# Weight sums in DRAM, in other groups and tied to other instructions, in a two-layer trunk

## The chip, the cores and the metric

One core of a Trainium2 chip runs the whole kernel. The metric is the device time of one execution in microseconds (us); lower is better. The engines are named as in the profile: PE (matmuls), PEld (PE's weight loads), DVE (vector), ACT (activation), POOL (general vector work, and here the issuer of software DMAs), SP (issuer of the loads). Each engine works through its own instruction queue in order, and waits for others by semaphores.

## The reference

The model has one sequence of 512 rows with 1024 features, and two layers. Layer 0 mixes with gated linear attention (queries, keys, values, gates and a decay, in chunks), layer 1 with a three-branch sparse attention (compressed, selected and windowed keys). Both add an attention over a memory of 256 rows, project the result with `w_out`, and then run a feed-forward part with a short convolution:

```python
h = h + jnp.concatenate([main.astype(xn.dtype), mo.astype(xn.dtype)], axis=-1) @ w_out[i]
h = h + conv_ffn(rmsnorm(h, norm_ffn[i]), w_up[i], conv_w[i], conv_b[i], w_down[i])
```

All is float32. The feed-forward part is `(silu(a) * b) @ w_down` with `a, b` the halves of the convolved `x @ w_up`, 2816 wide each.

## The kernel before

**Matmuls in three.** Every float32 factor is split into a high and a low part (ACT makes the high one, DVE the rest), and a product is three matmuls: high by high, low by high, high by low. Weights come in blocks of 128 x 1024 floats (512 KB): SP loads one (`wraw`), ACT and DVE split it (`wh`, `wl`), PE uses it. PE is given its order by hand wherever the code ties each matmul to the one before.

**Products with seven in place of eight.** Much of the two feed-forward parts multiplies 2 x 2 blocks with seven products instead of eight. These need sums of the four quarters of a weight block. The sums don't depend on the data, so the kernel lets POOL form them in DRAM by DMA beside the other work, in the array `qsum`. There are 35 such blocks, and each takes five transfers, which the code calls stages and this text calls **sums** alike:

- stages 0 and 1: a plain copy of two quarters each (512 KB) from the input `in_qd` to `qsum`;
- stage 2: two quarters of the input added to the first two (512 KB, an accumulating DMA);
- stages 3 and 4: one quarter of `qsum` added to another (256 KB each). Stage 3 needs stages 1 and 2, stage 4 needs stage 3.

`self.jobs` lists all 175 in order, in groups of blocks: stage 0 of each block of a group, then stage 1 of each, and so on. `pace(ins, n)` (line 284) takes the next `n` from the list, issues them on POOL's queue, and ties each to the instruction `ins` of another engine, so that it can't go out before. A sum that needs another waits on POOL for its landing, and there are eight semaphores for these DMAs in turn, so each also waits for the one eight places before. POOL's own work stands in the same queue: what is behind a waiting sum waits too.

**The order of the work**, with the calls of `pace` that matter here:

- Layer 0: queries and keys in six projections (`queries_keys`, line 706; from the fourth on two sums each); the memory's keys and values (two sums after each of two projections); the memory's two query projections (two each); the **value projection** `glav` beside the attention over the memory (one sum every eight steps, eight in all). Beside it POOL casts four pieces of the decays (`las`, line 759) for a DVE subtraction (line 761), which stands in DVE's queue ahead of work of the attention over the memory (`mP`).
- The gated linear attention in eight pieces (three sums each). POOL makes there the factor `oss` of a norm (lines 906 and 907), which DVE needs at line 911; behind that stand the merges `C`, and behind those ACT's copies `v` (line 900) that free PE's bank `po`.
- `w_out` (line 1023, line 1032 its matmuls) for layer 0, blocks 3 to 7: two sums each, tied to `low_ins`, the DVE instruction that has split the block's weights.
- The feed-forward part of layer 0, with sums tied to ACT's convolutions. Its start, and that of layer 1's, needs `rc` (line 426): DVE makes a mean of squares from PE's column sums, POOL raises it to the power -1/2, and PE transposes it (line 432) between two runs of 12 matmuls of the second up-projection.
- Layer 1: keys with four sums, the values of the sparse branches (`values` in `others`, line 2116, seven sums), then six double steps of scores and values. POOL multiplies the softmax weights `P` there (line 2061), which PE then transposes (line 1996).
- `w_out` for layer 1: eight blocks, two sums each, tied as above. Then the second feed-forward part and the output.

## Time and profile before

| what | value |
|---|---|
| time, median of 3 runs | 1247.51 us (1245.46 to 1250.63) |
| the profiled execution's own time | 1246.41 us |
| its span, first to last instruction | 1244.6 us |
| PE busy | 1217.1 us (98%) |
| DVE, ACT, POOL busy | 950.5, 694.4, 255.5 us |
| mean granted PE clock | 0.989 |
| software DMAs (the sums and two more) | 25408 packets, 75.74 MB |
| loads by SP | 61068 packets, 155.90 MB |

Rows of a timeline read: start, length, engine, line, instruction, out<-in, how many; in brackets the engine's idle time before it and what ended that. Rows of waits read: who waited for whom, us in total, times, the longest. Issuing a DMA on POOL is shown with the time that POOL spends on it, not with the transfer's. Line numbers are those of the kernel before; in the changed one those behind the list are three or four higher.

### The profile page before, as it was taken

Reading aid. Unit: us, or ns where it says so; the run is one execution under the profiler, and the core shown is the slowest. Engines: PE = TensorE matmul, PEld = TensorE weight load, DVE = VectorE, ACT = ScalarE, POOL = GpSimd, SP = SyncE. Lnnn points to the kernel's source line nnn. Section 1 sums busy time; section 2 is a strip of 40 time slices with the busy share of each in tenths; the row PEclk is TensorE's granted clock in tenths of the full one; section 3 lists DMA queues with packets and bytes.
Section 4 is the critical chain, followed back from the end, with each engine's and each line's share of the span. In section 5 each row is a group of like instructions: output and inputs, shape, how many; then the busy total and the mean of one; then the engine's idle time right before and its main releaser. Section 6 shows DMA issues by size and latency. Waiting matters only on the chain.

```text
span 1244.6 us, 20732 instructions
## 1 busy us (share of the span) xinstructions
PE 1217.1 (98%) x7657; PEld 1056.2 (85%) x7657; DVE 950.5 (76%) x1723; ACT 694.4 (56%) x1321; POOL 255.5 (21%) x356
## 2 busy tenths in 40 slices
PE   9989999999999999999999999699999999999998
PEld 6878788888889999899888788688888888988886
DVE  7755777689868888778768577685599888888785
ACT  7646455456545555556625677574456555555554
POOL 1221344210111110110122355673111111100000
PEclk9989989999999999999999999899999999999999
DMA  8786769966877876987765733733977988975544
GB/s 289 217 204 164 127 169 171 230 195 209 185 186 222 216 189 201 272 196 228 219 195 188 162 94 98 170 96 109 225 186 180 267 230 213 229 211 168 179 128 152
DMA packets 88385, 235.47 MB, mean 189 GB/s; under 512 B 10111, under 2 KB 13984, under 8 KB 87772
## 3 DMA queue, kind: packets, MB, share of 16 engines
q1 hardware_dynamic: 61068, 155.90, 39.3%
q0 software_dynamic: 25408, 75.74, 30.9%
q10 hardware_dynamic: 1808, 2.51, 0.6%
q8 instruction: 60, 0.98, 0.3%
q14 instruction: 41, 0.34, 0.1%
HBM read 222.01 MB, written 79.74 MB: 242 GB/s over the span
## 4 chain that ended last, share of the span: by engine, by line
PE 88%; DMA 5%; DVE 2%; ACT 1%; POOL 1%; issue 1%; SPq 0%; POOLq 0%; ACTq 0%; DVEq 0%
PE acc L1256 15%; PE acc L1152 11%; PE acc L1158 10%; PE acc L1032 5%; PE acc L385 4%; PE po L1995 3%; DMA qsum<-qsum 3%; PE sc L1332 3%; PE acc L1332 2%; PE po L1332 2%; PE sc L1521 2%; PE po L1521 2%; PE acc L1995 2%; PE acc L782 2%; PE acc L1521 2%; PE po L403 2%
## 5 line engine op out<-in xcount | busy, mean ns | idle before, releaser
L201 DVE TENSOR_TENSOR wl<-wraw,wh 128x1024 fp32r<-128x1024 f32 (+2 forms) x128 | 147.4, 1162 | 21.4 <-ACT wh L201 20.0
L201 ACT ACTIVATE wh<-wraw 128x1024 fp32r<-128x1024 f32 (+2 forms) x128 | 128.1, 1007 | 49.8 <-issue 14.8
L201 DVE SCALAR_TENSOR_TENSOR hc<-acc,taps,hc 128x511 f32<-128x511 f32 (+1 forms) x144 | 107.7, 748 | 48.2 <-ACT hc L201 45.9
L349 ACT ACTIVATE wh<-wraw 128x1024 fp32r<-128x1024 f32 x80 | 84.5, 1057 | 91.7 <-PE acc L1032 33.3
L350 DVE TENSOR_TENSOR wl<-wraw,wh 128x1024 fp32r<-128x1024 f32 x80 | 102.7, 1284 | 19.6 <-ACT wh L349 19.0
L282 POOL DMA_DIRECT2D qsum<-qsum x70 | 60.0, 913 | 240.0 <-ACT hc L201 104.7
L201 ACT ACTIVATE hc<-acc,taps 128x512 f32<-128x512 f32 x72 | 55.9, 777 | 91.5 <-DVE acc L201 38.2
L1256 PE MATMUL acc<-xh,wh 128*128 128x512 f32 x272 | 105.9, 390 | 0.0
L1256 PE MATMUL acc<-xh,wl 128*128 128x512 f32 x272 | 105.9, 389 | 0.0
L1256 PE MATMUL acc<-xl,wh 128*128 128x512 f32 x272 | 105.8, 389 | 0.0
L280 POOL DMA_DIRECT2D qsum<-in_qd x70 | 39.3, 563 | 275.8 <-ACT hc L201 163.3
L1152 PE MATMUL acc<-xl,wh 128*128 128x512 f32 x208 | 81.0, 389 | 0.0
L1152 PE MATMUL acc<-xh,wl 128*128 128x512 f32 x208 | 81.0, 389 | 0.0
L1152 PE MATMUL acc<-xh,wh 128*128 128x512 f32 x208 | 80.9, 389 | 0.0
L2061 POOL TENSOR_TENSOR P<-P,ssm 128x256 f32<-128x256 f32 (+3 forms) x48 | 64.9, 1373 | 1.8
L1256 PEld LDWEIGHTS acc<-xh,wh 128*128 128x128 f32 x272 | 51.1, 188 | 10.7 <-issue 0.4
L1256 PEld LDWEIGHTS acc<-xl,wh 128*128 128x128 f32 x272 | 51.1, 188 | 10.6
L1256 PEld LDWEIGHTS acc<-xh,wl 128*128 128x128 f32 x272 | 51.1, 188 | 10.3
L2053 ACT ACTIVATE P<-P,smn 128x128 f32<-128x128 f32 (+3 forms) x96 | 53.3, 557 | 10.1 <-DVE smn L2051 9.0
L282 POOL DMA_DIRECT2D qsum<-in_qd x35 | 29.5, 913 | 126.2 <-ACT hc L201 96.4
L1152 PEld LDWEIGHTS acc<-xl,wh 128*128 128x128 f32 x208 | 39.0, 188 | 8.2
L1152 PEld LDWEIGHTS acc<-xh,wl 128*128 128x128 f32 x208 | 39.0, 188 | 7.8
(631 smaller groups left out, 3816.3 us busy)
## 6 DMA issues: line engine op xcount, KB each, us to landing
wraw<-in_wp SPq DMA_DIRECT2D x122, 512.0 KB, 4.7
qsum<-in_qd POOLq DMA_DIRECT2D x105, 512.0 KB, 6.9
qsum<-qsum POOLq DMA_DIRECT2D x70, 256.0 KB, 7.3
wraw<-qsum SPq DMA_DIRECT2D x30, 512.0 KB, 5.3
wraw<-in_qd SPq DMA_DIRECT2D x30, 512.0 KB, 5.1
wraw<-qsum SPq DMA_DIRECT2D x51, 256.0 KB, 5.5
wraw<-in_qd SPq DMA_DIRECT2D x26, 256.0 KB, 4.3
strip<-vecd SPq DMA_DIRECT2D x12, 448.0 KB, 4.1
```

Source lines behind the costliest of these rows:

```text
L201: ins = f(*a, **kw)
L282: return self.nc.gpsimd.dma_start(to, what, accum_op=ALU.add)
L349: self.split_ins = nc.scalar.activation(wh, raw, AF.Copy)
L350: self.low_ins = nc.vector.tensor_tensor(out=wl, in0=raw, in1=wh.bitcast(F32), op=ALU.subtract)
L1032: nc.tensor.matmul(banks[m], a[:, o], b, start=k == 6 and i == 0, stop=k == 5 and i == 2)
L1152: pe(nc.tensor.matmul(dst, w[a][:, o], self.x[k][b], start=k + n == 0, stop=k == KC - 1 and n == 2))
L1158: pe(nc.tensor.matmul(dst, w[a][:, o], (X if n < 4 else T)[n][k][x], start=first and k + i == 0, stop=k == 3 and i == 2, skip_group_check= ...
L1256: pe(nc.tensor.matmul(pu[half], a[:, o], self.x[k][b], start=k == 0 and n == 0, stop=k == KC - 1 and n == 2))
L1332: pe(nc.tensor.matmul(dst, a[:, o], b, start=first and n == 0 and i % 2 == 0, stop=stop and n == 2, skip_group_check=True))
L1521: pe(nc.tensor.matmul(bank[i][:, c], a[:, ts], b[:, c], start=first and n == 0, stop=stop and n == 2, skip_group_check=True))
L1995: mm = lambda *args, **kw: pe(nc.tensor.matmul(*args, **kw))
L2061: nc.gpsimd.tensor_tensor(out=P, in0=P, in1=f[:, i, :].unsqueeze(2).to_broadcast([128, 2, 128 * t + 128]), op=ALU.mult)
```

## The change

Three edits. The first two groups of the list hold six blocks each (60 sums), all later ones three as before. The fourth of the query and key projections issues no sums. `w_out` ties its sums to the last matmul of the same block instead of to the split of its weights, and issues two per block in layer 0 and three per block in layer 1; the values of the sparse branches issue none.

```diff
--- before.py
+++ after.py
@@ -234,7 +234,10 @@
             for i, j in enumerate(FAST[l]):
                 blocks += [self.upb(l, j), self.downb(l, n - 1 + i)]
             blocks += [self.downb(l, p) for p in range(n - 1 + len(FAST[l]), NJ // 2)]
-        self.jobs = [(b, n) for i in range(0, len(blocks), 3) for n in range(5) for b in blocks[i:i + 3]]
+        self.jobs = []
+        while blocks:
+            some, blocks = blocks[:6 if len(self.jobs) < 60 else 3], blocks[6 if len(self.jobs) < 60 else 3:]
+            self.jobs += [(b, n) for n in range(5) for b in some]
 
     def t(self, pool, shape, tag, dt=F32, bufs=None):
         self.n += 1
@@ -710,7 +713,8 @@
                     else:
                         qp = self.ps("sc" if i == 3 else "acc")
                         self.projA(qp, self.wget(self.W[("glak", "glaq")[r]][j]))
-                        self.pace(self.move, 2)
+                        if i > 3:
+                            self.pace(self.move, 2)
                     sc = DK ** -0.5 if r else 1.0
                     for lo, hi, dst in ((0, DK, qk[:, :, r, j, :]), (DK, 128, qk[32 * j:32 * j + 32, :, r, 3, :])):
                         nc.vector.scalar_tensor_tensor(out=dst, in0=qp[lo:hi].rearrange("p (c t) -> p c t", c=4), scalar=sc,
@@ -1029,7 +1033,7 @@
             for k in ks:
                 o = slice(128 * k, 128 * k + 128)
                 for i, (a, b) in enumerate(((wh, main[k][0]), (wl, main[k][0]), (wh, main[k][1]))):
-                    nc.tensor.matmul(banks[m], a[:, o], b, start=k == 6 and i == 0, stop=k == 5 and i == 2)
+                    self.move = nc.tensor.matmul(banks[m], a[:, o], b, start=k == 6 and i == 0, stop=k == 5 and i == 2)
 
         ws, banks = {}, {}
         for m in range(lead):
@@ -1042,7 +1046,7 @@
                 banks[m] = self.ps("acc")
                 part(m, (6, 7))
             part(m, range(6))
-            self.pace(self.low_ins, 2)
+            self.pace(self.move, 2 + l)
             self.residual(m, banks[m], 4 + l)
 
 
@@ -2123,8 +2127,6 @@
                     for i, _ in enumerate(values()):
                         if i == 16:
                             run(q, 3)
-                        if i % 5 == 0:
-                            self.pace(self.move)
                         yield
                     c0 = compressed(0)
                     ahead_c.append(c0)
```

The program's order of instructions moves on POOL alone (on DVE one subtraction `las` changes places with two neighbours).

POOL, from the first sums to the casts of `las` in layer 0, before:

```order
L280 DMA qsum_81<-in_qd 128x1024 x6
L426 TENSOR_TENSOR rcm_544<-rcm_544,mhalf_110 128x2
L282 DMA qsum_81<-in_qd 128x1024 x3
L282 DMA qsum_81<-qsum_81 128x512 x6
L759 CAST las_121<-las_121 64x384
L280 DMA qsum_81<-in_qd 128x1024
L759 CAST las_121<-las_121 64x384
```

The same place now:

```order
L283 DMA qsum_81<-in_qd 128x1024 x4
L429 TENSOR_TENSOR rcm_542<-rcm_542,mhalf_110 128x2
L283 DMA qsum_81<-in_qd 128x1024 x8
L285 DMA qsum_81<-in_qd 128x1024
L763 CAST las_121<-las_121 64x384
L285 DMA qsum_81<-in_qd 128x1024
L763 CAST las_121<-las_121 64x384
```

Ahead of the first cast stood six copies, three sums of stage 2 and six of stages 3 and 4; now twelve copies and one sum of stage 2 stand there.

POOL in the fourth double step of the sparse attention, before (`Pc` and `cf` belong to the compressed branch, `ssm` and `P` to the softmax weights):

```order
L2089 TENSOR_TENSOR cf_8612<-cf_8612,gates_6344 128x8
L2090 TENSOR_TENSOR Pc_8487<-Pc_8487,cf_8612 128x256
L282 DMA qsum_81<-qsum_81 128x512 x3
L280 DMA qsum_81<-in_qd 128x1024
L282 DMA qsum_81<-qsum_81 128x512
L2058 TENSOR_TENSOR ssm_8536<-ssm_8536,gates_6344 128x4
L280 DMA qsum_81<-in_qd 128x1024
L2061 TENSOR_TENSOR P_1463_8537<-P_1463_8537,ssm_8536 128x512
L2061 TENSOR_TENSOR P_1474_8618<-P_1474_8618,ssm_8536 128x768
```

and now:

```order
L2093 TENSOR_TENSOR cf_8603<-cf_8603,gates_6342 128x8
L2094 TENSOR_TENSOR Pc_8478<-Pc_8478,cf_8603 128x256
L2062 TENSOR_TENSOR ssm_8527<-ssm_8527,gates_6342 128x4
L2065 TENSOR_TENSOR P_1463_8528<-P_1463_8528,ssm_8527 128x512
L2065 TENSOR_TENSOR P_1474_8609<-P_1474_8609,ssm_8527 128x768
L2076 MEMSET Pc_8780 128x8
```

The six sums between these products are gone; all sums of this part stand behind the last product.

POOL from the last products `P` to `rc` of the second feed-forward part, before:

```order
L2061 TENSOR_TENSOR P_1620_9214<-P_1620_9214,ssm_9213 128x512
L2061 TENSOR_TENSOR P_1625_9228<-P_1625_9228,ssm_9213 128x768
L280 DMA qsum_81<-in_qd 128x1024 x2
L282 DMA qsum_81<-in_qd 128x1024 x3
L282 DMA qsum_81<-qsum_81 128x512 x3
L426 TENSOR_TENSOR rc_9752<-rc_9752,mhalf_110 128x4
L282 DMA qsum_81<-qsum_81 128x512 x3
```

and now:

```order
L2065 TENSOR_TENSOR P_1620_9205<-P_1620_9205,ssm_9204 128x512
L2065 TENSOR_TENSOR P_1625_9219<-P_1625_9219,ssm_9204 128x768
L283 DMA qsum_81<-in_qd 128x1024 x4
L285 DMA qsum_81<-in_qd 128x1024 x3
L285 DMA qsum_81<-qsum_81 128x512 x6
L283 DMA qsum_81<-in_qd 128x1024 x6
L285 DMA qsum_81<-in_qd 128x1024 x3
L285 DMA qsum_81<-qsum_81 128x512 x2
L429 TENSOR_TENSOR rc_9751<-rc_9751,mhalf_110 128x4
L285 DMA qsum_81<-qsum_81 128x512 x4
```

Eight sums stood between the last `P` and `rc`; now 24 do.

## The prediction

> **What bounds the kernel now.** I read the engines' busy time first, then TensorE's waits, then who held the engine that was waited for.

> ```profile
> PE 1217.1 (98%) x7657; PEld 1056.2 (85%) x7657; DVE 950.5 (76%) x1723; ACT 694.4 (56%) x1321; POOL 255.5 (21%) x356
> ```

> PE is busy for 98% of the span. A change that moves only DMAs on POOL's queue can therefore win only from PE's few waits, and lose only by making new ones. The view of PE's waits has three that matter:

> ```profile
> PE pt L1996 <- POOL P L2061: 9.6, 1, 9.6
> PE pt L585 <- DVE mP L576: 4.7, 1, 4.7
> PE po L782 <- ACT v L900: 3.4, 1, 3.4
> ```

> The view by stretches, one stretch for each wait, from the last matmul before it to the end of the reduced clock behind it, gives the whole price (columns: length, then busy time of PE, PEld, DVE, ACT, POOL, then the granted clock, DMA share and GB/s):

> ```profile
> 81.55:90.41 8.86, 4.17 (x13) 3.50 (x13) 7.09 (x14) 2.83 (x10) 1.05 (x3) 0.62 0.75 151
> 152.58:162.09 9.51, 6.11 (x19) 5.14 (x19) 6.69 (x27) 4.54 (x16) 3.87 (x8) 0.64 0.75 165
> 797.21:810.63 13.42, 3.78 (x13) 3.19 (x14) 3.95 (x12) 3.52 (x13) 6.41 (x9) 0.62 0.93 208
> ```

> Length less PE busy is the wait: 4.69, 3.40 and 9.64 us. PE's work after each wait runs at half clock (a granted 0.62 to 0.64 over a stretch is half for most of it), so half of the 4.17, 6.11 and 3.78 us is lost too: 2.1, 3.05 and 1.9. I call them A (6.8 us), B (6.45) and C (11.5); together **24.8 us**.

> All three lead to POOL. For A and B the waits of DVE name it:

> ```profile
> DVE las L761 <- POOL las L759: 6.9, 1, 6.9
> DVE v L911 <- POOL oss L907: 6.4, 2, 6.0
> ```

> POOL runs its queue in order, and a weight sum whose earlier stage has not landed holds whatever stands behind it. POOL's timeline at A, at B and at C:

> ```profile
> 51.69 1.79 POOL L282 DMA_DIRECT2D qsum<-in_qd  x2 [0.21 <-issue]
> ...
> 63.35 0.81 POOL L282 DMA_DIRECT2D qsum<-qsum  x1 [7.38 <-DMA qsum<-in_qd]
> 67.24 0.84 POOL L282 DMA_DIRECT2D qsum<-qsum  x1 [3.07 <-DMA qsum<-in_qd]
> 71.51 0.82 POOL L282 DMA_DIRECT2D qsum<-qsum  x1 [3.43 <-DMA qsum<-in_qd]
> 75.02 0.81 POOL L282 DMA_DIRECT2D qsum<-qsum  x1 [2.69 <-DMA qsum<-qsum]
> 77.47 0.81 POOL L282 DMA_DIRECT2D qsum<-qsum  x1 [1.64 <-DMA qsum<-qsum]
> 80.22 0.83 POOL L282 DMA_DIRECT2D qsum<-qsum  x1 [1.94 <-DMA qsum<-qsum]
> 81.10 0.50 POOL L759 CAST las<-las 64x384 fp32r<-64x384 f32 x1
> ...
> 147.81 0.81 POOL L282 DMA_DIRECT2D qsum<-qsum  x1 [2.02 <-DMA qsum<-qsum]
> 148.69 0.19 POOL L906 TENSOR_SCALAR oss<-oss 128x2 f32<-128x2 f32 x1
> ...
> 793.84 2.51 POOL L282 DMA_DIRECT2D qsum<-qsum  x3
> ...
> 803.41 0.81 POOL L282 DMA_DIRECT2D qsum<-qsum  x1 [6.51 <-DMA qsum<-qsum]
> ...
> 805.74 2.48 POOL L2061 TENSOR_TENSOR P<-P,ssm 128x512 f32<-128x512 f32 x2
> ```

> At A the cast that DVE needs stands behind nine sums in which each third waits for the one three places ahead. At B the factor `oss` stands behind the same kind of wait. At C one sum waits 6.51 us, and the product P that PE is to transpose stands behind it.

> **The change part by part.** *Groups of six* (the first 60 sums). A sum now needs a stage issued six or more places earlier. The cast of `las` stands behind 13 sums: eight plain copies of stages 0 and 1, which wait for nothing but their matmuls, four copies that wait for the copy eight places before, and one sum of stage 2, which waits for the fifth copy. That one goes out where POOL stands at 51.69 now, and has until 71 to land. None is a sum of the stages 3 and 4 that hold POOL from 63.35 to 80.22. POOL comes to the cast when the first matmuls of the value projection release the sum before it, right behind the second query projection, whose result DVE reads at 71.10:

> ```profile
> 71.10 0.69 DVE L497 SCALAR_TENSOR_TENSOR qf<-sc,rb 128x512 f32<-128x512 f32 x1 [0.35 <-PE sc L385]
> ```

> So the cast comes at some 72 to 73 instead of 81.10. DVE begins to wait for it at about 74.7 (its wait of 6.9 ends with the cast, at 81.6). So A goes: **-6.8**. At B the sums ahead of `oss` are of stages 3 and 4, but their sources were all issued in the value projection, two pieces of work earlier. POOL then makes `oss` as soon as ACT has its squares, and DVE's 6.0 us wait, longer than PE's 3.4, goes: **-6.45**. It isn't paid back by blocks that come too late: the first formed block is read at 257.7, and its last needed stage is then the 19th of 175 sums, issued in the value projection. At the end the last sum goes out at 1098.7 and the last formed block is read at 1140.1, 41 us later.

> ```profile
> L282 POOL DMA_DIRECT2D qsum<-qsum x70: 805/824/1477, 63.3 to 1098.7; - x70
> ...
> L291 SPq DMA_DIRECT2D wraw<-qsum x9: 319/327/327, 257.7 to 1140.1; - x9
> ```

> *No sums at the fourth projection, none beside the sparse values.* Two and seven sums fewer at those places. They cost PE nothing there, so I count 0. Every sum behind them is two places later in the first feed-forward part and one in the second, some 5 to 10 us of the 41 just named.

> *Second output projection*: 24 sums instead of 16, each three tied to the end of a block's own matmuls, not to the split of its weights, which had run ahead into the attention. So no sum stands between the products P: C goes, **-11.5**.

> But all 24 now stand between the last P and `rc` of the second feed-forward part. There POOL had 14.30 us to spare:

> ```profile
> 862.38 1.07 POOL L280 DMA_DIRECT2D qsum<-in_qd  x2 [11.50 <-DVE wl L350]
> 866.51 1.70 POOL L282 DMA_DIRECT2D qsum<-in_qd  x2 [3.07 <-DVE wl L350]
> 870.60 0.81 POOL L282 DMA_DIRECT2D qsum<-in_qd  x1 [2.40 <-DVE wl L350]
> 877.51 0.83 POOL L282 DMA_DIRECT2D qsum<-qsum  x1 [6.10 <-DMA qsum<-in_qd]
> ...
> 886.42 0.81 POOL L282 DMA_DIRECT2D qsum<-qsum  x1 [3.02 <-DMA qsum<-in_qd]
> 901.53 1.03 POOL L426 TENSOR_TENSOR rc<-rc,mhalf 128x4 f32<-128x4 f32 x1 [14.30 <-DVE rc L425]
> ```

> and PE needs `rc` soon after it can be made, since its transposes stand between two runs of 12 matmuls (the chain of waits: start, length, what):

> ```profile
> 856.49 7.25 PE acc L1032 x31
> ...
> 867.82 27.20 PE acc L1032 x120
> 895.02 5.44 PE acc L1256 x24
> 901.25 2.89 PE acc L385 x12
> 904.57 2.76 PE acc L385 x12
> ```

> The first block's 18 matmuls end at about 859.5 (half of the 36 that end at 863.6), the last block's at 895.0. How long do 24 sums take? They queue in the DMA engines one behind another, so I price each kind by the distance of two landings. Stage 2 (512 KB added): 67.24 to 63.35 and 71.51 to 67.24, 4.1 us; here, 877.51 to 886.42 for two, 4.45. Stages 3 and 4 (256 KB added): 75.02, 77.47, 80.22, so 2.6. Copies (512 KB), from three that went out 0.5 us apart at 931.8:

> ```profile
> DMA to landing us min/median/max: 5.6/6.7/8.3
> ```

> (8.3 - 5.6 + 1.0) / 2 = 1.85 us, with 3.7 us ahead of the first. The last sum before `rc` may go out when the sum three places ahead, the 21st, has landed. These 21 are 10 copies, 5 of stage 2 and 6 of stages 3 and 4: 18.5 + 20.5 + 15.6 = 54.6 us. With 3.7 from 859.5 that is 917.8; the issue (0.82) and `rc` (1.03) end at 919.7. PE is free at 904.1 (901.25 + 2.89), so it waits **15.6 us**, and loses about 2.3 behind it at half clock (mean of 2.1, 3.05 and 1.9): **+17.9**. Nothing fills this hole: every matmul left needs `rc`'s row or stands behind it.

> Bounds: all software transfers of the POOL queue together (packets, MB, share of the span) show

> ```profile
> q0 software_dynamic: 25408, 75.74, 30.9%
> ```

> which is 384.6 us for 177 transfers, 2.17 us each, against 2.6 for my mix of 15 sums (38.9 / 15). At that rate 54.6 becomes 45.6 and the wait 6.6. With 4.45 for stage 2 and 10% more for the rest it is 59.8, and the wait 20.8. I take the middle because the rows at 63 to 80 and at 866 to 886 have the same mix of sums and weight loads. [...]

> The sum against the profiled execution's own 1246.41: 1246.4 - 6.8 - 6.45 - 11.5 + 17.9 = **1239.6 us**. That execution is 1.1 us under the median of 1247.51, of which the forecast is 0.6% less.

> **The rivals.** *The sums drain in time.* If the 21 need under 38.3 us (901.5 - 859.5 - 3.7), `rc` isn't late: 1246.4 - 24.8 = 1221.6. For it: the loads of the next weights stop once PE stands, which frees the engines. Against: it needs 30% less than the rows. [...]

> *Groups of six don't free the cast and `oss`.* If POOL is as late as now at A and B, only C is won: 1246.4 - 11.5 + 17.9 = 1252.8. For it: twelve copies now stand close together at 43 to 71, beside the weight loads. Against: none of the sums ahead of the cast needs a source younger than 8 places.

> *Slower: the DMA engines are overbooked.* At the second feed-forward part's start, just behind 895.0, SyncE stores h, when copies and stage-2 sums are still queued:

> ```profile
> spill<-h SPq DMA_DIRECT2D x2, 2048.0 KB, 7.9
> ```

> If its 7.9 us fall wholly on the sums and these are at their upper price, the wait is 20.8 + 7.9 = 28.7, and with 2.3 the total 1246.4 - 24.8 + 31.0 = 1252.6; from a wait of about 29 us on (24.8 + 6.2 - 2.3) the change is over 0.5% slower. For it: the store starts when the queue is longest. Against: engines that are fully asked for have not starved PE's loads so far,

> ```profile
> 60.00:80.00 20.00, 20.00 (x92) 16.62 (x91) 9.81 (x13) 12.11 (x18) 4.10 (x5) 1.00 1.03 259
> ```

> with a DMA share of 1.03 and PE busy throughout. If the overbooked engines also brought each of the five blocks' weights 2 us late, it would be 1262.6.

> **How the numbers follow.** Forecast (three waits go, one comes) 0.60, with its own range 1230 (a wait of 6.6) to 1245 (20.8, and a little of A or B left); drained in time 0.16; A and B stay 0.13; slower 0.11. About 0.5%, 6.2 us, is what a measurement of this kernel can tell from no change, so the edge is 1240.2 on the scale of the profiled execution. The forecast lies on it: 0.34 below, 0.26 above. Faster 0.34 + 0.16 = 0.50; same 0.26 + 0.11 (most of "A and B stay") = 0.37; slower the rest, 0.13. The range 1225 to 1251 reaches into the drained case and leaves out its end and the slower ones.

> **What would show it.** PE's waits should no longer name mP, v L900 or P; the granted clock near 83, 155 and 800 us should be full. POOL's `rc` should be preceded by a sum that waits for "DMA qsum<-in_qd", and PE's longest wait should be the transposes of `rc` at some 880 us of the new span, 7 to 21 us long. If `rc` waits for DVE again, the queue's price was wrong, and the time is near 1222. If `las` or `oss` still holds DVE, the part on groups of six was.

## The result, and the profile after

The changed kernel takes 1263.36 us (median of 4 runs, 1260.92 to 1264.42), the kernel before 1248.32 (1245.46 to 1250.63) beside it: a ratio of 1.0119, 95% interval 1.0092 to 1.0145. It is 1.2% slower. The forecast was 1239.6, 0.6% faster, and the time lies above the range of 1225 to 1251. The profiled execution took 1264.42 with a span of 1262.6, 18.0 more than the span before.

The page's line of busy time and its row of the granted clock, after the change:

```profile
PE 1214.4 (96%) x7657; PEld 1054.4 (84%) x7657; DVE 952.2 (75%) x1723; ACT 694.1 (55%) x1321; POOL 255.8 (20%) x356
...
PEclk9999999999999999999999999999789999999999
```

PE has lost two points of its share; the clock's row dips in one place, about 900 us (its slices are too long for the shorter dip at 250). The view of PE's waits says what for (total, times, longest):

```profile
PE pt L435 <- POOL rc L429: 34.9, 2, 25.9
PE pt L1923 <- DVE hid L1972: 1.8, 1, 1.8
PE pt L2000 <- ACT PT L2167: 1.3, 1, 1.3
```

The three waits A, B and C no longer name mP, v and P. In their place PE waits twice for `rc`, not once: 9.0 us at the first feed-forward part, 25.9 at the second. I call them E and D. The view by stretches, from the last matmul before each to the end of the reduced clock behind it:

```profile
244.89:257.85 12.96, 3.97 (x13) 3.29 (x13) 2.19 (x4) 1.40 (x2) 2.73 (x3) 0.60 0.89 235
894.70:923.45 28.75, 2.86 (x9) 2.48 (x10) 1.02 (x2) 0.88 (x2) 5.18 (x6) 0.58 1.01 241
```

Behind both waits the granted clock is 0.50 until the end of the stretch. So E costs 8.99 us and half of the 3.97 behind it, 11.0 in all; D 25.89 and half of 2.86, **27.3**. The account of the two spans: A, B and C gone, -24.8; 1.3 of C left; D +27.3; E +11.0; and 3.5 for `hid` (a wait of 1.8, and 1.7 as half of the 3.41 us behind it, at a granted 0.50). That is +18.3, against 18.0 measured.

POOL's timeline shows who stands in front of `rc`. At the first feed-forward part:

```profile
214.45 1.75 POOL L285 DMA_DIRECT2D qsum<-in_qd  x2 [18.01 <-PE acc L1036]
219.87 0.81 POOL L285 DMA_DIRECT2D qsum<-in_qd  x1 [3.66 <-PE acc L1036]
224.45 0.81 POOL L285 DMA_DIRECT2D qsum<-in_qd  x1 [3.77 <-issue]
230.03 0.81 POOL L285 DMA_DIRECT2D qsum<-qsum  x1 [4.77 <-issue]
234.31 0.81 POOL L285 DMA_DIRECT2D qsum<-qsum  x1 [3.46 <-issue]
240.13 0.81 POOL L285 DMA_DIRECT2D qsum<-qsum  x1 [5.01 <-issue]
...
251.94 0.82 POOL L285 DMA_DIRECT2D qsum<-qsum  x1 [3.88 <-issue]
252.49 1.34 POOL L429 TENSOR_TENSOR rc<-rc,mhalf 128x4 f32<-128x4 f32 x1
```

and at the second:

```profile
850.59 1.64 POOL L283 DMA_DIRECT2D qsum<-in_qd  x3 [9.16 <-PE acc L1036]
...
869.34 0.81 POOL L285 DMA_DIRECT2D qsum<-qsum  x1 [8.55 <-DMA qsum<-in_qd]
...
918.65 0.81 POOL L285 DMA_DIRECT2D qsum<-qsum  x1 [3.74 <-DMA qsum<-in_qd]
919.20 1.34 POOL L429 TENSOR_TENSOR rc<-rc,mhalf 128x4 f32<-128x4 f32 x1
```

Two things are to be seen. In both places `rc`, a product of 1.0 to 1.3 us, follows right behind a sum. Before, POOL had 14.30 us to spare at the second, and 9.96 at the first:

```profile
256.42 1.04 POOL L426 TENSOR_TENSOR rc<-rc,mhalf 128x4 f32<-128x4 f32 x1 [9.96 <-DVE rc L425]
```

And many of the first part's waits are put down to "issue" and not to a transfer. The sum of stage 3 at 230.03 adds what the sum six places ahead brought, which had landed at 201.35, and the matmul that it is tied to had ended at 224.9. It goes out all the same only at 230.03, 0.9 us after the sum *three* places ahead landed (229.10). That is no wait of the program; I put it down to the queue itself. Without it the last of the ten, at 251.94, could have left by 240: its tie had ended at 235.8, and its source had landed at 237.8.

I counted this in the trace of every kernel here: for each adding sum, how many adding sums were on their way (issued, and the last packet of their completion not yet seen) when it went out, itself included.

```
adding sums on their way, the new one included     1    2    3    4 or more
before                                            33   36   36    0
after                                             30   45   30    0
```

With a copied sum counted as one and an adding sum as two, no sum of any kernel went out at more than seven, and 7 did at exactly seven in the kernel before and 7 in the changed one; a whole adding sum never went out as a fourth. The fullest mixes of whole sums were three adding and one copied, two and three, one and five. The program's eight semaphores are not this limit: they would let eight go, of either kind. The theory that I then tested: **POOL's queue holds about three adding sums, and whoever stands behind the fourth waits for the oldest to land. What the change loses is only POOL's order in front of the two `rc`.** The rivals: the DMA engines are overbooked wherever the sums stand; the store of h at the second feed-forward part makes the sums slow; the groups of six in themselves make `rc` late.

### The profile page after: what moved, and what is told of

Same layout as the page of the kernel before. It is cut to its first block, busy times and chain, and to the rows that moved or that the text cites. A ratio compares the mean times of both kernels' runs of the same rounds, so it can differ in the third digit from the quotient of the medians.

```text
span 1262.6 us, 20739 instructions
## 1 busy us (share of the span) xinstructions
PE 1214.4 (96%) x7657; PEld 1054.4 (84%) x7657; DVE 952.2 (75%) x1723; ACT 694.1 (55%) x1321; POOL 255.8 (20%) x356
## 3 DMA queue, kind: packets, MB, share of 16 engines
q0 software_dynamic: 25408, 75.74, 31.1%
q10 hardware_dynamic: 1808, 2.51, 0.7%
## 4 chain that ended last, share of the span: by engine, by line
PE 89%; DMA 4%; issue 3%; DVE 2%; ACT 1%; POOL 1%; SPq 0%; POOLq 0%; ACTq 0%; DVEq 0%
PE acc L1260 14%; PE acc L1156 11%; PE acc L1162 10%; PE acc L786 4%; PE acc L388 4%; DMA qsum<-in_qd 4%; PE po L1999 3%; PE po L406 3%; PE acc L1036 3%; PE sc L1336 2%; PE po L1336 2%; PE acc L1336 2%; PE sc L1525 2%; PE po L1525 2%; PE acc L1999 2%
## 5 line engine op out<-in xcount | busy, mean ns | idle before, releaser
L1260 PEld LDWEIGHTS acc<-xh,wl 128*128 128x128 f32 x272 | 51.1, 188 | 10.3
```

Of the source, the lines that this page charges most:

```text
L1260: pe(nc.tensor.matmul(pu[half], a[:, o], self.x[k][b], start=k == 0 and n == 0, stop=k == KC - 1 and n == 2))
```

## The experiments

**Groups of six alone.** The kernel before with only the new list of sums:

```diff
-        self.jobs = [(b, n) for i in range(0, len(blocks), 3) for n in range(5) for b in blocks[i:i + 3]]
+        self.jobs = []
+        while blocks:
+            some, blocks = blocks[:6 if len(self.jobs) < 60 else 3], blocks[6 if len(self.jobs) < 60 else 3:]
+            self.jobs += [(b, n) for n in range(5) for b in some]
```

> The kernel before with the groups of six for the first twelve blocks and nothing else of the change. Theory (POOL's order in front of rc sets the loss, and the later ties put the sums there): A and B go (6.8 + 6.45 us), C stays (11.5), and rc of both feed-forward parts is in time, since the sums of the output projections still follow the splits of the weights, which run ahead: 1248.3 - 13.3 = about 1235 us. Rival (groups of six alone make the first rc late, because six sums of stage 2 now stand one behind another there): A and B go, but 11 us come back at the first rc: about 1246 us.

Measured: 1244.85 us, ratio 0.9983 (0.9970 to 0.9996), only 2.7 us of the 13. Its view of PE's waits, and POOL's timeline ahead of the new wait:

```profile
PE pt L1999 <- POOL P L2064: 9.3, 1, 9.3
PE pt L786 <- DVE v L914: 7.7, 1, 7.7
```

```profile
194.16 0.89 POOL L285 DMA_DIRECT2D qsum<-in_qd  x1 [2.00 <-issue]
199.44 0.82 POOL L285 DMA_DIRECT2D qsum<-in_qd  x1 [4.38 <-issue]
203.06 0.81 POOL L285 DMA_DIRECT2D qsum<-in_qd  x1 [2.81 <-issue]
203.94 0.19 POOL L909 TENSOR_SCALAR oss<-oss 128x2 f32<-128x2 f32 x1
```

A and B are gone, and neither `rc` is late, so the groups of six alone are not what makes E. But six sums of stage 2 come one after another around a later `oss`, and a new wait of 7.7 us comes at 198 us (9.7 by an estimate, with as much lost at half clock behind it as the 2.0 us behind E). Neither side had seen that; POOL issues the last three of the six with two adding sums on their way each time, so it is the queue's limit again. The wait for `hid` is here too, with 1.9 us.

**The ties and counts alone.** The changed kernel with groups of three (the diff above, reversed).

> The changed kernel with groups of three throughout: only the ties and counts of the sums differ from the kernel before. Theory: C goes (-11.5 us), A and B stay, the second rc is late by about 26 us as in the changed kernel (27.3 with the half clock behind it): about 1264 us. If the late rc of the second feed-forward part needed the groups of six ahead of it (rival), it would be in time here: about 1237 us.

Measured: 1265.19 us, ratio 1.0138 (1.0116 to 1.0159).

```profile
PE pt L432 <- POOL rc L426: 26.3, 1, 26.3
PE pt L585 <- DVE mP L576: 4.0, 1, 4.0
...
PE po L783 <- ACT v L901: 1.4, 1, 1.4
```

This is what the theory said. D is there in full without a single group of six ahead of it, and C is gone. A is back with 4.0 us; of B 1.4 us is back at its place, and 2.5 us come at an `oss` 50 us later. At the first feed-forward part six of POOL's ten sums are now copies, and it is done in time:

```profile
244.65 0.52 POOL L280 DMA_DIRECT2D qsum<-in_qd  x1 [4.40 <-PE acc L1033]
...
250.12 1.71 POOL L282 DMA_DIRECT2D qsum<-in_qd  x2 [3.82 <-PE acc L1033]
256.19 1.04 POOL L426 TENSOR_TENSOR rc<-rc,mhalf 128x4 f32<-128x4 f32 x1 [4.37 <-DVE rc L425]
```

So E needs both halves of the change: the ten adding sums that the groups of six bring to that place, and the ties or counts (a run below shows that it is the tie). D comes from the ties and counts alone.

**The sums behind `rc`.** The changed kernel with these two lines:

```diff
-            self.pace(self.move, 2 + l)
+            if l and m < 3:
+                self.pace(self.move, 3)
...
-            self.pace(self.conv_ins, 2 + l)
+            self.pace(self.conv_ins, (5, 8)[l] if j < 3 else 2 + l)
```

> The changed kernel with the sums of both output projections moved behind rc: none in the first projection (10 sums less), three at each of the first three blocks of the second (9 instead of 24), and in the first three steps of the feed-forward parts 5 and 8 sums each instead of 2 and 3. As many sums, the same computation. Theory (the loss is only POOL's order in front of rc): both waits for rc go, 11.0 and 27.3 us: 1263.4 - 38.3 = about 1225 us. Rival (the DMA engines are overbooked, wherever the sums stand): the sums collide with the weights of the first blocks of the feed-forward parts, PE waits there instead, and half or less of the 38 us is won: 1244 us or more.

Measured: 1238.01 us, ratio 0.9930 (0.9910 to 0.9950): 25 us below the changed kernel, two thirds of the 38.

```profile
PE acc L1157 <- DVE hc L201: 6.3, 4, 2.1
PE acc L1261 <- ACT hc L201: 2.0, 1, 2.0
```

```profile
880.44 1.03 POOL L429 TENSOR_TENSOR rc<-rc,mhalf 128x4 f32<-128x4 f32 x1 [20.56 <-DVE rc L428]
```

Both waits for `rc` are gone, with as many sums in the program. The rival holds for a part: PE now waits, 7.0 us in all between 979 and 1032 us, for blocks whose weights arrive late (two of their loads took 17 and 20 us) beside the sums that were moved there.

**Without the store of h** in the second feed-forward part. The kernel leaves the store out, and loads a part of the input where h was to come back:

```diff
-            nc.sync.dma_start(spill, flat(self.hs))
+            if l == 0:
+                nc.sync.dma_start(spill, flat(self.hs))
...
-            queue.dma_start(flat(self.hs), spill)
+            queue.dma_start(flat(self.hs), spill if l == 0 else self.I["xp"][:, 136:136 + KC * S])
```

> The changed kernel without the 2 MB store of h at the start of the second feed-forward part; what is loaded back there later is a part of the input instead, so this part of the computation is left out. Theory (the seven copies in front of the second rc took 2.6 us each instead of 1.85 because they shared the DMA engines with this store): the wait of 25.9 us shrinks by 5 to 9 us, the time to 1254 to 1258 us. Rival (the transfers inside DRAM cost this much whatever runs beside them): less than 2 us, 1262 us or more.

Measured: 1265.65 us, ratio 1.0148 (1.0131 to 1.0164). The wait does not shrink:

```profile
PE pt L435 <- POOL rc L429: 36.1, 2, 28.5
```

The six copies that share their time with the store landed in 14.2 us instead of 18.1, but the fifteen other sums up to the 21st took 55.1 instead of 49.2. The store is not what makes D long.

**Two sums per block in the second output projection**, not three:

```diff
-            self.pace(self.move, 2 + l)
+            self.pace(self.move, 2)
...
-            self.pace(self.conv_ins, 2 + l)
+            self.pace(self.conv_ins, 6 if l and j < 3 else 2 + l)
```

> The changed kernel with two sums per block in the second output projection instead of three (16 instead of 24), and the eight others in the first three steps of the second feed-forward part (6 each instead of 3). Same computation. Theory (each sum in front of rc costs what lies between two landings, 67.3 us for 21 of them, 3.2 each): the second wait shrinks from 25.9 to 0 to 5 us, and the time by 22 to 27 us, to 1237 to 1241. Rival (POOL is late by the last few sums alone, or by something that does not depend on their number): the wait stays above 12 us.

Measured: 1243.45 us, ratio 0.9961 (0.9945 to 0.9977).

```profile
PE pt L435 <- POOL rc L429: 9.8, 1, 9.8
PE sc L1525 <- ACT sh L201: 3.6, 1, 3.6
```

Only E is left of the waits for `rc`: eight sums less have taken away all 25.9 us of D, at least 3.2 us each. The time is 2.5 us above the expected range; a new wait of 3.6 us stands where the eight sums went, behind a load of weights that took 10.6 us.

**The old tie, everything else as changed:**

```diff
-            self.pace(self.move, 2 + l)
+            self.pace(self.low_ins, 2 + l)
```

> The changed kernel with the sums of both output projections tied to the splits of the weights, as in the kernel before, with 2 and 3 per block. Theory (the later tie puts the sums in front of the first rc, and the earlier one puts them between the products P): the first wait for rc (9.0 us, 11.0 with the half clock) goes, C comes back with 9.6 us or a little more (11.5), and of the second wait part goes, since the first sums leave during the attention: 1245 to 1263 us. Rival (the mix of sums that the groups of six bring there makes the first rc late): the first wait stays at 7 to 9 us.

Measured: 1240.75 us, ratio 0.9940 (0.9919 to 0.9962), below the expected range. One name in one line is worth 22.6 us, and together with the first two runs it shows that E needs the later tie as well as the groups of six.

```profile
PE pt L787 <- DVE v L915: 4.7, 1, 4.7
PE pt L2000 <- POOL P L2065: 3.8, 1, 3.8
PE sc L1999 <- DVE smn L2055: 2.4, 1, 2.4
```

```profile
249.20 1.02 POOL L429 TENSOR_TENSOR rc<-rc,mhalf 128x4 f32<-128x4 f32 x1 [5.93 <-DVE rc L428]
...
888.86 0.81 POOL L285 DMA_DIRECT2D qsum<-qsum  x1 [4.24 <-DMA qsum<-in_qd]
895.70 1.03 POOL L429 TENSOR_TENSOR rc<-rc,mhalf 128x4 f32<-128x4 f32 x1 [6.03 <-DVE rc L428]
```

Both `rc` are made when DVE has its part ready: I had expected only a part of D to go, but the 24 sums now start at 788 us and are through in time. C comes back, smaller (3.8 and 2.4 us), because the sums stand between the products P again; and 4.7 us are lost to an `oss` at 199 us, as with the groups of six alone.

**What does the queue count?** The changed kernel with each adding sum as two transfers of 64 rows:

```diff
-        return self.nc.gpsimd.dma_start(to, what, accum_op=ALU.add)
+        return [self.nc.gpsimd.dma_start(to[o:o + 64], what[o:o + 64], accum_op=ALU.add) for o in (0, 64)]
```

> The changed kernel with each adding sum as two transfers of 64 rows instead of one of 128; the same bytes and the same computation, 105 issues more. In all runs so far no adding sum went out while more than two others were on their way. Theory A (the queue holds a number of rows, and an added row counts twice a copied one): up to six or seven halves are on their way at once, as many bytes as before, and the time stays within 5 us of the changed kernel's 1263.4. Theory B (the queue holds three adding transfers, of whatever size): three halves, half of the bytes in flight, POOL clears its queue later, and the second wait for rc grows by 10 us or more: 1273 us or above.

Measured: 1258.93 us, ratio 1.0090 (1.0065 to 1.0114). The same count as above, with halves:

```
adding halves on their way, the new one included   1    2    3    4    5    6    7    8 or more
                                                  24   56   41   44   22   17    6    0
```

**Spread.** What these runs say together: put the sums where nothing small and urgent stands behind them on POOL, and not all in one place. The changed kernel with

```diff
-            self.pace(self.move, 2 + l)
+            if l and m < 3:
+                self.pace(self.move, 4)
...
-            self.pace(self.conv_ins, 2 + l)
+            self.pace(self.conv_ins, 5 if j < 3 else 2 + l)
...
                             run(q, 3)
+                        if i % 5 == 0:
+                            self.pace(self.move)
```

> The changed kernel with the sums spread so that no row of them stands in front of an rc and the first blocks of the second feed-forward part have no backlog: the seven sums beside the sparse values are put back, the first output projection has none, the second has four at each of its first three blocks (12 instead of 24), and the first three steps of both feed-forward parts have five each. Same computation. Theory: both waits for rc stay away as with 9 sums there (POOL had 20.6 us to spare before that rc, three more sums cost 8), and the waits that came instead at 979 to 1032 us (7.0 us in all) shrink, since about ten sums fewer are due there: 1228 to 1233 us. Rival (those waits come from the sums of the feed-forward part itself): no change from 1238 us.

Measured: 1231.37 us, ratio 0.9869 (0.9844 to 0.9894), in the expected range. The waits at 979 to 1032 us are gone; PE does not wait beside the sparse values, where seven sums stand again. What is left at the head of PE's waits:

```profile
PE acc L1261 <- ACT sh L201: 2.1, 1, 2.1
PE acc L1261 <- ACT hc L201: 2.0, 1, 2.0
```

The chain of waits puts both down to one load of a formed block, in the stretch where POOL issues fifteen sums:

```profile
256.79 11.84 DMA wraw<-qsum
```

**Six sums back in front.** From the kernel of the run before:

```diff
-            if l and m < 3:
-                self.pace(self.move, 4)
+            self.pace(self.move, (4 if m < 3 else 0) if l else {3: 4, 5: 2}.get(m, 0))
...
-            self.pace(self.conv_ins, 5 if j < 3 else 2 + l)
+            self.pace(self.conv_ins, (3, 5)[l] if j < 3 else 2 + l)
```

> The kernel of the run before (sums spread) with six of the fifteen early sums of the first feed-forward part moved back in front of it: four at the first block of the first output projection and two at the third, and three instead of five in each of the first three steps. Same computation. The view of the run before has PE wait 4.1 us at 270 to 277 us for a formed block whose load was on its way for 11.8 us while fifteen sums ran. Theory (with at most three adding sums on their way, six there leave POOL free by 229, before rc can be made at 242, and the load is faster): those 4.1 us and about 1 of half clock go: 1231.4 - 5 = about 1226.5 us. Rival (a load of a formed block costs this with any sums beside it): no change, 1231.

Measured: 1229.02 us, ratio **0.9846 (0.9824 to 0.9867)**: 1.5% faster than the kernel before. It is the lowest median here, 2.5 us above the expected one, and not clear of the run before, since the two intervals overlap. What the trace shows is that the two waits at 270 to 277 us are gone, and that the loads of formed blocks between 240 and 300 us took at most 8.7 us instead of 11.8. PE's longest waits now:

```profile
PE pt L1923 <- DVE hid L1972: 1.9, 1, 1.9
PE sc L1525 <- ACT sh L201: 1.8, 2, 1.2
```

POOL still runs into the queue's limit, but with nothing urgent behind it. Three adding sums go out together, three more as others land (POOL stands for 7.37 and 5.06 us), and `rc` still waits for DVE:

```profile
214.00 2.60 POOL L285 DMA_DIRECT2D qsum<-in_qd  x3 [18.00 <-PE acc L1036]
223.97 0.81 POOL L285 DMA_DIRECT2D qsum<-in_qd  x1 [7.37 <-issue]
...
233.81 0.81 POOL L285 DMA_DIRECT2D qsum<-qsum  x1 [3.17 <-DVE xl L201]
...
241.84 1.02 POOL L429 TENSOR_TENSOR rc<-rc,mhalf 128x4 f32<-128x4 f32 x1 [6.98 <-DVE rc L428]
```

**The same with groups of three** (the first diff, reversed):

> The same kernel with groups of three throughout. Theory (what the groups of six bring is not that sources are older, but that copies and not adding sums stand in front of the cast of las, and that fewer adding sums stand in front of oss): A and B come back, 13 us: about 1240 us. Rival (the tie and the spreading alone bring the gain): within 3 us of the same kernel with groups of six.

Measured: 1240.02 us, ratio 0.9936 (0.9911 to 0.9960), 11.0 us above the same kernel with groups of six.

```profile
PE pt L585 <- DVE mP L576: 4.6, 1, 4.6
PE po L783 <- ACT C L872: 2.4, 2, 2.1
```

A is back in full; of B only a wait of 2.1 us shows, 50 us later, behind `oss` again. This profiled execution (1234.73) is the fastest of six, so its view shows less than the median lost. The groups of six are worth their place, though the reason that I gave was not the whole one.

## Why the prediction was wrong, step by step

**What bounds the kernel** was right: PE's few waits, all by way of POOL's order. With those waits and the new ones gone the kernel runs at 1229.0, 7 us above the 1221.6 that the forecast named for a kernel without A, B, C and D.

**A and B: right in size, with a reason that was not the whole one.** The cast of `las` was to come at 72 to 73 us and came at 73.38; `oss` is no longer late at 150:

```profile
73.38 0.83 POOL L763 CAST las<-las 64x384 fp32r<-64x384 f32 x1
...
143.04 2.60 POOL L285 DMA_DIRECT2D qsum<-qsum  x3 [1.76 <-PE po L786]
145.72 0.33 POOL L910 TENSOR_SCALAR oss<-oss 128x2 f32<-128x2 f32 x1
```

The prediction had seen that copies would stand in front of the cast. But the step "A sum now needs a stage issued six or more places earlier" made me think that adding sums would no longer hold POOL. They do, by threes, whatever their sources, as the sum at 230.03 shows. The old groups hid this: with groups of three, the sum that a sum depends on *is* the one three places ahead, so the queue's limit and the program's dependence end together and the profile names the transfer. By the count, A was won because copies, which weigh half, came to stand in front of the cast, and B because the sums ahead of `oss` went out by threes, each time into a queue with at most one left in it. That is read from the traces; no run changed the age of the sources alone.

**The first feed-forward part is the step that failed outright.** The prediction has no term for the later tie in the first output projection. Of the first feed-forward part it wrote only that every sum "is two places later", and set this against the 41 us that the last formed blocks have to spare: a cost of 0. It asked who reads the sums, and not what stands behind them on POOL. The same `rc` that it priced in the second part stands in the first, with 10 us of slack before. The later tie and ten adding sums in front of it made E: **+11.0**.

**D: the mechanism was right, a term was mis-sized.** The forecast was a wait of 15.6 us (17.9 with the half clock), and 7 to 21 as its range; it is 25.9 (27.3). Term by term, for the 21 sums from the issue of the first to the landing of the last:

```
                              forecast   measured
first four copies (+ start)     11.1       12.1
three of stage 2                12.3       13.4
six of stages 3 and 4           15.6       15.6
six copies                      11.1       18.1
two of stage 2                   8.2        8.1
sum                             58.3       67.3
```

The wait was forecast 10.3 us too short. The term that failed is the six copies, with 7.0 of these: 1.85 us each came from three that left one behind another into an empty queue. Behind six adding sums the six took 3.0 each. The first four copies and the first three sums of stage 2 took about 1 us more each time. Of the rest, 0.5 is the start (the first sum left 44.1 us before PE ran out, not 44.6) and 0.8 the last issue and `rc`. The upper bound of 20.8 was drawn from the same 1.85 with 10% on it; that bound was too near. What sets a copy's price between 1.85 and 3.0 stays open: without the store of h the six copies took 14.2 us, but the others took more.

**C** went to 1.3 us, a wait of another kind, and the half clock behind it is gone (a granted 1.00 from 799 to 802 us, where it was 0.50 from 806.85 to 810.6 before): -10.2 where -11.5 was forecast. The wait for `hid` (3.5 us with what follows) was not foreseen. It stands in seven of the twelve profiles here, with 1.7 to 1.9 us, and in five not (one has 0.3 us); what brings it was not tried.

**The rivals.** "The sums drain in time" and "A and B stay" are refuted. "The DMA engines are overbooked" came nearest in size, with a wait of 28.7 us, but not by its mechanism: the store of h is not the cause, and the same number of sums placed elsewhere takes both waits away. That its last figure, 1262.6, lies close to the measured time is luck: it had weights that come late in the place of E. The misses add up: 11.0 for E, 9.4 for D, 1.3 for C and 3.5 for `hid` are 25.2, and 1239.6 + 25.2 = 1264.8, against the profiled 1264.42.

## What to carry to other kernels

Before work is added to a queue that runs in order, list everything small that stands behind it on the same engine, at every place where the pattern recurs, and take the slack of each; here the same `rc` was priced at one place and overlooked at the other. Where a wait and a dependence end together, the profile cannot tell a limit of the queue from the program's own order: count the transfers on their way before a dependence is loosened. And take the price of a transfer in a quiet stretch as a lower bound, not a middle, for the same transfer in a full queue: here it was 1.85 us against 3.0.

## What the runs showed of the hardware

With a copied row counted as one and an added row as two, in units of 128 rows, none of more than 2,100 sums in the twelve profiles went out with more than seven units on their way, itself included, and 111 went out at exactly seven. The weights are those that fit the counts; a limit of the queue is read from them. POOL stood idle meanwhile: 4.77 us before the sum at 230.03, which no wait of the program held. In the changed kernel nine idle times of POOL before such a sum, 31.5 us in all, are put down to "issue":

```profile
POOL qsum L285 <- issue: 31.5, 9, 5.0
```

(the changed kernel's view of POOL's waits). And splitting each adding sum into halves, with 105 issues more, did not show as slower: 1.0090 of the time before against 1.0119, intervals that overlap.
